# Decay sums of the Mamba heads: from selecting matmuls in PSUM to broadcast loads through DRAM into SBUF

## The chip, the cores and the metric

The kernel runs on one core of one Trainium2 chip, in one launch. The time is the device time of the whole kernel in microseconds, the median of several runs. TensorE (PE in the rows; PEld are its weight loads), VectorE (DVE), ScalarE (ACT), GpSimd (POOL) and SyncE (SP) each work off their own instructions in the order in which the program was built. SP asks for nearly all transfers from memory, ACT for a few.

## The reference

Two layers of a decoder trunk on 256 tokens of width 1024: first a hybrid of gated linear attention and sparse attention and a dense SwiGLU, then a Mamba-2 mixer and eight SwiGLU experts of which each token takes two. The change lies in the Mamba mixer. Of it, this matters:

```
dt = jax.nn.softplus(dt.astype(jnp.float32) + dt_bias)
A = -jnp.exp(a_log.astype(jnp.float32))
a = (dt * A).reshape(B, NC, Q, G, R).transpose(0, 3, 4, 1, 2)
cum = jnp.cumsum(a, axis=-1)
seg = cum[..., :, None] - cum[..., None, :]
L = jnp.exp(jnp.where(causal, seg, -jnp.inf))
cb = jnp.einsum('bclgn,bcsgn->bgcls', Cc, Bc)
y_diag = jnp.einsum('bgcls,bgrcls,bcsgrp->bclgrp', cb, L, xdt)
```

There are 32 heads in four groups of eight. For each head, the running sum cum of its decays is wanted along the tokens on every partition, so that the differences seg of all pairs of tokens can be made. The kernel works in chunks of 128 tokens, two of them, which gives the same y.

## The kernel before

**Stages.** The hybrid mixer runs to about 175 us of the profiled execution, the dense SwiGLU to 378, the Mamba stage to some 600, then the experts. Their first matmul (L1313) starts at 608.8 and they take the rest of the time.

**Weights.** Every weight comes as a tile of 1 MB named raw, asked for by SP at L238 in load(). The tiles form a ring: pool raw_p, to which raw2 is added ahead of the dense stage and raw3 ahead of the experts. A load waits until the tile of one round earlier has been read. Up to the experts, split() makes of each half of a tile a rounded high part wh (ACT, L252) and the remainder wl (DVE, L253), and a product takes three matmuls: wh with the high part of the activations (L267), with their low part (L268), wl with the high part (L269).

**The Mamba stage.** At its start, L963 to L968 make cum, a tile of 32 heads x 256 tokens named fo. L970 to L974 store it as a high and a low part, chl, and make pick. For each of the four groups g of heads, s_proj(g) computes three pairs of projections (each pair in a PSUM bank pa), runs a conv over them (conv(): ACT L986, then three rows on DVE, L988), then the pairs of projections for the gate zs, two tiles, and the activations of xbc (L1019) and zs (L1021), each behind a load of ACT's function table. s_core(g) runs over j = 0 to 3, two heads each. cums(j) puts their running sums on all partitions: two matmuls at L1052 that pick a row of chl, into a PSUM bank pb. ACT reads that bank for seg (four activations, L1066) and for fo (L1069) and takes the exponential of seg (L1070), DVE multiplies both (L1073, L1075), TensorE makes y of them in six matmuls 64 x 128 (L1080 to L1082), DVE adds and multiplies with zs (L1083, L1085). After j = 3 comes the norm of the group: the square y on ACT (L1088), four matmuls (L1091), a copy ms (L1093), one matmul (L1096) and the scaling of y (L1101). L1031, L1032 and L1042 are the first matmuls of the next group's core. outs() runs the output projection on finished groups: y_split() makes hh on ACT (L1115) and yl on DVE (L1116), out_proj() 128x512 matmuls with them.

**What sets the order.** The string SSM_ORDER gives the order in which the steps of these generators are written (p is s_proj, c is s_core). A scheduler then orders each engine's instructions on its own estimates of their times, under the dependences and the free buffers. So an edit at one place can move instructions of all engines of a stage.

Of the kernel before, what the change touches and what calls it, by code (L numbers as in the profile page):

```python
# [8 lines left out]
F32 = mybir.dt.float32  # L9
BF16 = mybir.dt.bfloat16  # L10
F32R = mybir.dt.float32r
# [5 lines left out]
D, T, KD = 1024, 256, 8  # L17
# [168 lines left out]
def trunk_kernel(ctx: ExitStack, tc: tile.TileContext, d: dict, out: bass.AP):  # L186
# [10 lines left out]
    def pbank(tag):  # L197
        return ps_p.tile([128, 512], F32, name=tag, bufs=4 if tag == "pa" else 2)
# [16 lines left out]
    def K(n):  # L215
        s, w = _CS[n]
        return cs[:, s:s + w]
# [679 lines left out]
        dgs = [g[1] for g in dgs]  # L897


    raws.append((ctx.enter_context(tc.tile_pool(name="raw2", bufs=3, side="right")), 3))  # L900
    late = ctx.enter_context(tc.tile_pool(name="late", bufs=1, side="right"))
    px = ctx.enter_context(ExitStack())
    part_p = px.enter_context(tc.tile_pool(name="part", bufs=2))
# [49 lines left out]
    with ExitStack() as sx:  # L953
# [13 lines left out]
        cum = sw.tile([32, T], F32, name="fo")  # L967
        V.tensor_tensor_scan(cum, resets(sw, 32, T, 128, "seg"), dx_, 0.0, op0=OP.mult, op1=OP.add)  # L968

        chl = sp.tile([64, T], F32R, name="chl")  # L970
        S.copy(chl[:32], cum)
        V.tensor_sub(chl[32:], cum, chl[:32].bitcast(F32))
        pick = sp.tile([64, 32], F32R, name="pick")
        S.copy(pick, K("sel32")[:64])  # L974
        dtd = sw.tile([32, 128], F32, name="ms", bufs=1)
        act(dtd, cum[:, :128], AF.Exp, bias=cum[:, 127:128], scale=-1.0)
        V.tensor_mul(dtd, dtd, dtv[:, :128])
# [49 lines left out]
        def s_core(g):  # L1027
# [18 lines left out]
                                 tk[:, i, 8 * g:8 * g + 8, None].to_broadcast([128, 8, 64]))  # L1046

            def cums(j):
                pcu = pbank("pb")
                for e in range(2):  # L1050
                    hh = 8 * g + 2 * j + e
                    PE.matmul(pcu[:, e * T:(e + 1) * T], pick[:, hh:hh + 1].to_broadcast([64, 128]), chl,  # L1052
                              start=True, stop=True)
                return pcu

            y = xT
            pcu = cums(0)
# [3 lines left out]
            for j in range(4):  # L1061
                h0 = 8 * g + 2 * j
                sg = sw.tile([128, 2, 2, 128], F32, name="seg")
                for e in range(2):
                    for c in range(2):
                        act(sg[:, e, c], pcu[:, e * T + c * 128:e * T + (c + 1) * 128], AF.Relu,  # L1066
                            bias=tk[:, 2 + c, h0 + e:h0 + e + 1], scale=-1.0)
                fo = sw.tile([128, 2, 128], F32, name="fo")
                act(fo, pcu.rearrange("p (e n) -> p e n", e=2)[:, :, 128:], AF.Exp)  # L1069
                act(sg, sg, AF.Exp, scale=-1.0)  # L1070
                if j < 3:
                    pcu = cums(j + 1)
                V.tensor_mul(sg.rearrange("p e c n -> p e (c n)"), sg.rearrange("p e c n -> p e (c n)"),  # L1073
                             cbm[:, 0:2].rearrange("p c n -> p (c n)")[:, None, :].to_broadcast([128, 2, 256]))
                V.tensor_mul(fo, fo, cbm[:, 2:3].to_broadcast([128, 2, 128]))  # L1075
                yield
                py = pbank("pc")
                for e in range(2):
                    o_, cc = slice(64 * e, 64 * e + 64), slice(128 * j + 64 * e, 128 * j + 64 * e + 64)
                    PE.matmul(py[o_, :128], xd[:, 0, cc], sg[:, e, 0], start=True, stop=True)  # L1080
                    PE.matmul(py[o_, 128:T], xd[:, 1, cc], sg[:, e, 1], start=True, stop=False)
                    PE.matmul(py[o_, 128:T], xd[:, 2, cc], fo[:, e], start=False, stop=True)  # L1082
                V.scalar_tensor_tensor(y[:, j], xT[:, j], P("dsk")[:, 4 * g + j:4 * g + j + 1], py[:, :T],  # L1083
                                       op0=OP.mult, op1=OP.add)
                V.tensor_mul(y[:, j], y[:, j], zs[:, j])  # L1085
                yield
# [98 lines left out]
    ax.close()  # L1185


    raws.append((ctx.enter_context(tc.tile_pool(name="raw3", bufs=7, side="right")), 7))
    with ExitStack() as mx:
        mp = mx.enter_context(tc.tile_pool(name="moe", bufs=1))  # L1190
        mw = mx.enter_context(tc.tile_pool(name="moew", bufs=2))
# [463 lines left out]
```

## Time and profile before

| | us |
|---|---|
| three runs | 1455.31, 1457.79, 1457.96 |
| median | 1457.79 |
| profiled execution, whole | 1458.05 |
| its span | 1456.0 |
| TensorE busy in the span | 1420.0 (98%) |
| DVE, ACT busy | 561.1 (39%), 437.5 (30%) |
| moved by DMA | 493.66 MB, mean 339 GB/s |

All times in the rows are us from the start of the span, unless ns is written. A row in order of time gives start, duration, engine, line, operation, output<-input with shapes and the number of instructions (x4); in brackets stands the idle time ahead and what ended it. Two rows of one engine may overlap, since its instructions are pipelined: what one costs in a chain is the distance from its start to the next one's. A row of a table by stretches gives the stretch, its length, then busy time and instructions of PE, PEld, DVE, ACT and POOL, then the granted TensorE clock (1.00 is 2.4 GHz, 0.50 is 1.2 GHz), the share of the DMA engines' time and GB/s. A matmul that stands in TensorE's queue and waits may count as busy, so that the distances of starts tell more than the share.

### The profile page before, as it was taken

To read this page: it belongs to the slowest core of one execution; us is meant where nothing else is said; L and a number is where in the kernel's file an instruction comes from. 1 tells how busy PE (TensorE), PEld (TensorE's weight loads), DVE (VectorE), ACT (ScalarE), POOL (GpSimd) and SP (SyncE) were. 2 spreads that over 40 slices of the span, in tenths; PEclk is the share of its full clock that TensorE was granted. 3 is DMA by queue.
4 is the path that set the end of the run, shared out by engine and by line. 5 is a ranking of instruction groups with operands and counts; after the bars stand their busy time and mean duration, and the time that the engine had idled before them with its cause. 6 is when DMAs were issued, how large, how long until landed. Compare 5 with 4: busy or idle time off the path is not lost. (4 is left out here: it accounts for less than half of the span.)

```text
span 1456.0 us, 28571 instructions
## 1 busy us (share of the span) xinstructions
PE 1420.0 (98%) x12257; PEld 808.6 (56%) x12257; DVE 561.1 (39%) x1096; ACT 437.5 (30%) x859; POOL 2.8 (0%) x11
## 2 busy tenths in 40 slices
PE   7999999999999999999999999999999999999996
PEld 6866699999799987633433333333334333333322
DVE  6888588875678778610110011010110110100101
ACT  5577454444577686311100011000001000000002
POOL 0000000000000000000000000000000000000000
PEclk9989999999999999999999999999999999999998
DMA  9876788986643433799999999999999999999994
GB/s 382 350 264 244 296 300 328 376 300 242 242 145 121 170 132 129 278 408 348 356 411 421 419 420 420 419 421 420 420 420 421 419 420 420 420 420 420 420 421 182
DMA packets 68964, 493.66 MB, mean 339 GB/s; under 512 B 7648, under 2 KB 7904, under 8 KB 9568
## 3 DMA queue, kind: packets, MB, share of 16 engines
q1 hardware_dynamic: 68544, 491.25, 84.2%
q8 instruction: 98, 1.61, 0.4%
q10 hardware_dynamic: 288, 0.52, 0.1%
q14 instruction: 34, 0.28, 0.0%
HBM read 490.70 MB, written 1.05 MB: 338 GB/s over the span
## 5 line engine op out<-in xcount | busy, mean ns | idle before, releaser
L1313 PE MATMUL pa<-raw,gx 128*32 128x512 f32 (+1 forms) x5120 | 506.6, 540 | 0.0
L1313 PEld LDWEIGHTS pa<-raw,gx 128*32 128x32 f32 x5120 | 167.0, 110 | 300.1 <-issue 262.5
L1313 PE MATMUL pb<-raw,at 128*32 128x512 f32 x2240 | 252.6, 594 | 0.5 <-ACT at L1348 0.5
L1481 DVE TENSOR_TENSOR sg<-sg,pa 128x256 f32<-128x256 f32 (+1 forms) x80 | 31.0, 387 | 476.5 <-ACT sg L1480 474.8
L253 DVE TENSOR_TENSOR wl<-raw,wh 128x1024 fp32r<-128x1024 f32 (+1 forms) x155 | 185.3, 1203 | 58.4 <-ACT wh L252 58.2
L252 ACT CAST wh<-raw 128x1024 fp32r<-128x1024 f32 (+1 forms) x155 | 158.9, 1035 | 121.0 <-PE pb L268 53.0
L1313 PEld LDWEIGHTS pb<-raw,at 128*32 128x32 f32 x2240 | 70.7, 110 | 152.3 <-issue 147.4
L1480 ACT ACTIVATE sg<-pa 128x256 f32<-128x256 f32 (+1 forms) x80 | 28.5, 357 | 348.5 <-PE pa L1313 348.5
L267 PE MATMUL pa<-hh,wh 128*128 128x256 f32 (+1 forms) x392 | 113.6, 292 | 1.4 <-ACT hh L380 0.6
L268 PE MATMUL pa<-hl,wh 128*128 128x256 f32 (+1 forms) x392 | 112.8, 288 | 0.8 <-DVE hl L386 0.8
L269 PE MATMUL pa<-hh,wl 128*128 128x256 f32 (+1 forms) x392 | 112.5, 288 | 0.0
L267 PE MATMUL pb<-hh,wh 128*128 128x256 f32 (+1 forms) x360 | 102.1, 284 | 1.9 <-ACT hh L380 1.9
L268 PE MATMUL pb<-hl,wh 128*128 128x256 f32 (+1 forms) x360 | 102.4, 285 | 0.1
L269 PE MATMUL pb<-hh,wl 128*128 128x256 f32 (+1 forms) x360 | 102.1, 284 | 0.0
L1348 ACT COPY at<-pc 128x512 f32<-128x512 f32 (+2 forms) x32 | 17.5, 545 | 262.6 <-PE pb L1313 135.1
L281 DVE SCALAR_TENSOR_TENSOR junk<-raw,scb 128x1024 bf16<-128x1024 f32 x72 | 87.7, 1218 | 1.7 <-DMA raw<-in_hyb_mod_dram 1.1
L267 PEld LDWEIGHTS pa<-hh,wh 128*128 128x128 f32 (+1 forms) x392 | 75.0, 192 | 5.4 <-issue 1.8
L268 PEld LDWEIGHTS pa<-hl,wh 128*128 128x128 f32 (+1 forms) x392 | 75.6, 193 | 2.1 <-DVE hl L386 0.9
L269 PEld LDWEIGHTS pa<-hh,wl 128*128 128x128 f32 (+1 forms) x392 | 75.3, 193 | 0.8 <-DVE gu L629 0.3
L267 PEld LDWEIGHTS pb<-hh,wh 128*128 128x128 f32 (+1 forms) x360 | 68.6, 191 | 2.9 <-ACT hh L380 2.1
L268 PEld LDWEIGHTS pb<-hl,wh 128*128 128x128 f32 (+1 forms) x360 | 68.7, 191 | 1.2 <-DVE hl L386 0.8
L269 PEld LDWEIGHTS pb<-hh,wl 128*128 128x128 f32 (+1 forms) x360 | 68.6, 191 | 0.3
(432 smaller groups left out, 1471.6 us busy)
## 6 DMA issues: line engine op xcount, KB each, us to landing
raw<-in_e_gu_dram SPq DMA_DIRECT2D x192, 1024.0 KB, 18.4
raw<-in_e_dn_dram SPq DMA_DIRECT2D x112, 1024.0 KB, 19.4
raw<-in_e_gl_dram SPq DMA_DIRECT2D x32, 1024.0 KB, 17.8
raw<-in_d_gu_dram SPq DMA_DIRECT2D x22, 1024.0 KB, 7.8
raw<-in_s_in_dram SPq DMA_DIRECT2D x20, 1024.0 KB, 4.8
raw<-in_hyb_mod_dram SPq DMA_DIRECT2D x12, 1024.0 KB, 9.4
raw<-in_ssm_mod_dram SPq DMA_DIRECT2D x12, 1024.0 KB, 6.9
raw<-in_d_dn_dram SPq DMA_DIRECT2D x11, 1024.0 KB, 8.3
```

What stands on the lines that cost most here:

```text
L252: hi_last[0] = S.copy(hi[:, :n], r)
L253: lo_last[0] = V.tensor_sub(lo[:, :n], r, hi[:, :n].bitcast(F32))
L267: PE.matmul(ps, a[0], b[0], start=start, stop=False, **kw)
L268: PE.matmul(ps, a[0], b[1], start=False, stop=False, **kw)
L269: return PE.matmul(ps, a[1], b[0], start=False, stop=stop, **kw)
L281: V.scalar_tensor_tensor(jk, r[:, q * D:(q + 1) * D], 1.0, scb, op0=OP.mult, op1=OP.mult, accum_out=macc[m][:, 2 * j + q:2 * j + q + 1])
L1313: up_last[0] = PE.matmul(ps[32 * j:32 * j + 32, :rhs.shape[1]], lhs, rhs, start=start, stop=stop)
L1348: (V.tensor_copy if i else S.copy)(at[:, i:i + n].rearrange("p a n -> p (a n)"), pt_[:, :n * 128])
L1480: last = act(sg[:, r, :w], pg[r][:, :w], AF.Silu)
L1481: V.tensor_mul(sg[:, r, :w], sg[:, r, :w], pg[r][:, w:2 * w])
```

## The change

cum is written once to a tile dr in DRAM and read back, four heads at a time, as a tile cb of 128 partitions x 1024 elements in which every partition holds the same four running sums. There are eight such loads of 512 KB into two buffers; ACT asks for the write and for all loads, the first two at the start, one more after each odd j. seg and fo read cb in SBUF in place of the bank pb. chl, pick and the 32 matmuls of cums go. raw2 has two tiles for three (eight tiles of 1 MB in the ring up to the experts for nine), raw3 eight for seven (sixteen as before in the experts).

```diff
-    raws.append((ctx.enter_context(tc.tile_pool(name="raw2", bufs=3, side="right")), 3))
+    raws.append((ctx.enter_context(tc.tile_pool(name="raw2", bufs=2, side="right")), 2))
...
-        chl = sp.tile([64, T], F32R, name="chl")
-        S.copy(chl[:32], cum)
-        V.tensor_sub(chl[32:], cum, chl[:32].bitcast(F32))
-        pick = sp.tile([64, 32], F32R, name="pick")
-        S.copy(pick, K("sel32")[:64])
+        dr = sx.enter_context(tc.tile_pool(name="dr", bufs=1, space=bass.MemoryType.DRAM)).tile([32, T], F32, name="dr")
+        S.dma_start(dr, cum)
+        cbs = []
+
+        def cum_load():
+            i = len(cbs)
+            if i < 8:
+                cbs.append(sp.tile([128, 4 * T], F32, name="cb", bufs=2))
+                S.dma_start(cbs[i], dr[4 * i:4 * i + 4].rearrange("h n -> (h n)")[None, :].to_broadcast([128, 4 * T]))
+
+        cum_load()
+        cum_load()
...
             def cums(j):
-                pcu = pbank("pb")
-                for e in range(2):
-                    hh = 8 * g + 2 * j + e
-                    PE.matmul(pcu[:, e * T:(e + 1) * T], pick[:, hh:hh + 1].to_broadcast([64, 128]), chl,
-                              start=True, stop=True)
-                return pcu
+                return cbs[2 * g + j // 2][:, j % 2 * 2 * T:(j % 2 + 1) * 2 * T]
...
                 act(sg, sg, AF.Exp, scale=-1.0)
+                if j % 2:
+                    cum_load()
                 if j < 3:
                     pcu = cums(j + 1)
...
-    raws.append((ctx.enter_context(tc.tile_pool(name="raw3", bufs=7, side="right")), 7))
+    raws.append((ctx.enter_context(tc.tile_pool(name="raw3", bufs=8, side="right")), 8))
```

Line numbers after the change are up to 7 higher: L988 becomes L995, L1066 to L1070 become L1068 to L1072, L1080 to L1096 become L1084 to L1100, L1115 becomes L1119. The built program shows that the order of the instructions in the Mamba stage moves too. Numbers behind a tile's name tell buffers apart; they differ between the two programs.

**DVE in the conv of the last group.** pa_5353 and pa_5444 are two of its three PSUM banks, wl_5617 is the first low part of the weights for the gate's projections that follow. Before:

```order
L988 SCALAR_TENSOR_TENSOR xbc_5351<-pa_5353,pc_69,xbc_5351 128x253
L988 SCALAR_TENSOR_TENSOR xbc_5351<-pa_5444,pc_69,xbc_5351 128x255
L253 TENSOR_TENSOR wl_5617<-raw_5614,wh_5616 128x1024
L988 SCALAR_TENSOR_TENSOR xbc_5351<-pa_5353,pc_69,xbc_5351 128x255
L988 SCALAR_TENSOR_TENSOR xbc_5351<-pa_5444,pc_69,xbc_5351 128x254
L988 SCALAR_TENSOR_TENSOR xbc_5351<-pa_5353,pc_69,xbc_5351 128x254
L988 SCALAR_TENSOR_TENSOR xbc_5351<-pa_5444,pc_69,xbc_5351 128x253
L988 SCALAR_TENSOR_TENSOR xbc_5351<-pa_5353,pc_69,xbc_5351 128x253
L1073 TENSOR_TENSOR seg_5600<-seg_5600,cbm_5423 128x512
L988 SCALAR_TENSOR_TENSOR xbc_5351<-pa_5444,pc_69,xbc_5351 128x255
```

After, with pa_5340, pa_5428 and pa_5505 as the three banks and wl_5597 as that low part:

```order
L995 SCALAR_TENSOR_TENSOR xbc_5338<-pa_5428,pc_69,xbc_5338 128x255
L995 SCALAR_TENSOR_TENSOR xbc_5338<-pa_5340,pc_69,xbc_5338 128x254
L995 SCALAR_TENSOR_TENSOR xbc_5338<-pa_5428,pc_69,xbc_5338 128x254
L995 SCALAR_TENSOR_TENSOR xbc_5338<-pa_5340,pc_69,xbc_5338 128x253
L995 SCALAR_TENSOR_TENSOR xbc_5338<-pa_5428,pc_69,xbc_5338 128x253
L995 SCALAR_TENSOR_TENSOR xbc_5338<-pa_5505,pc_69,xbc_5338 128x254
L1089 TENSOR_TENSOR xbc_4920<-xbc_4920,zs_4921 128x256
L995 SCALAR_TENSOR_TENSOR xbc_5338<-pa_5505,pc_69,xbc_5338 128x253
L253 TENSOR_TENSOR wl_5597<-raw_5594,wh_5596 128x1024
L253 TENSOR_TENSOR wl_5625<-raw_5594,wh_5624 128x1024
```

The low part stood among the rows of the first two banks; now it stands behind the last row but one of the third.

**TensorE where group 2 is handed over to group 3.** hh_4418 and hh_4421 are the activations of the output projection. Before:

```order
L269 MATMUL pa_5964<-wh_5987,yl_5966 128x512
L267 MATMUL pa_5965<-wh_5987,hh_4418 128x512
L268 MATMUL pa_5965<-wl_5988,hh_4418 128x512
L269 MATMUL pa_5965<-wh_5987,yl_5966 128x512
L1091 MATMUL pc_5787<-y_5785,cs_68 32x256 x4
L268 MATMUL pa_5963<-wl_6006,hh_4418 128x512
L269 MATMUL pa_5963<-wh_6005,yl_5966 128x512
L267 MATMUL pa_5964<-wh_6005,hh_4418 128x512
L1096 MATMUL pc_5794<-ms_5792,cs_68 128x256
L1031 MATMUL pc_5808<-xbc_5351 128x256
L1032 MATMUL pc_5808<-xbc_5351 128x128
```

After:

```order
L1084 MATMUL pc_5755<-seg_5743,xd_5414 64x128
L1085 MATMUL pc_5755<-seg_5743,xd_5414 64x128
L1086 MATMUL pc_5755<-fo_5748,xd_5414 64x128
L1095 MATMUL pc_5766<-y_5764,cs_68 32x256 x4
L1100 MATMUL pc_5773<-ms_5771,cs_68 128x256
L1038 MATMUL pc_5787<-xbc_5338 128x256
L1039 MATMUL pc_5787<-xbc_5338 128x128
L1049 MATMUL pc_5795<-cs_68,xbc_5338 128x128 x4
L267 MATMUL pa_5929<-wh_5938,hh_4421 128x512
L268 MATMUL pa_5929<-wl_5939,hh_4421 128x512
L267 MATMUL pa_5930<-wh_5938,hh_4421 128x512
```

L1091 stood in a row of wide matmuls of the output projection, 28 of them behind the last L1082; its counterpart L1095 now follows the last L1086 at once, and the wide matmuls begin behind L1100 and L1049.

**ACT at the same place.** zs_5352 and zs_5339 are the gate of group 3, y_5785 and y_5764 the squares of group 2. Before:

```order
L1115 CAST hh_4418<-y_4808 128x1024
L1066 ACTIVATE seg_5863<-pb_5840,tk_4089 128x128 x4
L1069 ACTIVATE fo_5868<-pb_5840 128x256
L1070 ACTIVATE seg_5863<-seg_5863 128x512
L252 CAST wh_6021<-raw_6003 128x1024
L1021 ACT_TABLE_LOAD
L1021 ACTIVATE zs_5352<-pa_5613 128x512
L1021 ACTIVATE zs_5352<-pa_5694 128x512
L348 ACT_TABLE_LOAD
L1088 ACTIVATE y_5785<-xbc_4931 128x1024
L1115 CAST hh_4418<-y_5328 128x1024
L1093 COPY ms_5792<-pc_5787 128x256
```

After:

```order
L1068 ACTIVATE seg_5808<-cb_5589,tk_4092 128x128 x4
L1071 ACT_TABLE_LOAD
L1071 ACTIVATE fo_5813<-cb_5589 128x256
L1028 ACT_TABLE_LOAD
L1028 ACTIVATE zs_5339<-pa_5593 128x512
L1028 ACTIVATE zs_5339<-pa_5671 128x512
L348 ACT_TABLE_LOAD
L1092 ACTIVATE y_5764<-xbc_4920 128x1024
L1072 ACTIVATE seg_5808<-seg_5808 128x512
L1068 ACTIVATE seg_5836<-cb_5589,tk_4092 128x128 x4
L1097 COPY ms_5771<-pc_5766 128x256
L1071 ACTIVATE fo_5841<-cb_5589 128x256
```

The cast hh for the output projection stood ahead of the gate and the square; now it follows them (two rows below the last one shown), and seg of group 3 stands ahead of them, with three table loads among these rows for two.

## Rows read from the trace of the kernel before

**Rows 1.** Table by stretches (columns as told above): Mamba, experts' first part, experts' long part.

```profile
510.00:552.00 42.00, 42.00 (x300) 36.23 (x298) 32.48 (x60) 35.33 (x61) 0.00 (x0) 1.00 0.35 125
611.00:740.00 129.00, 129.00 (x1411) 48.25 (x1407) 16.51 (x63) 14.85 (x37) 0.00 (x0) 1.00 0.96 376
780.00:1440.00 660.00, 651.21 (x6383) 232.28 (x6379) 66.86 (x152) 56.90 (x134) 0.00 (x0) 1.00 1.00 415
```

**Rows 2.** Waits of SP's DMA queue, 611 to 740 us: line, releaser, us, times, longest.

```profile
SPq L238 <- PE pa L1313: 82.0, 35, 9.8
```

**Rows 3.** TensorE in order of time around a pair of L1052 among projections.

```profile
513.74 0.28 PE L269 MATMUL pa<-hh,wl 128*128 128x256 f32 x1
513.95 0.50 PE L1052 MATMUL pb<-chl,pick 64*128 64x256 f32 x2
514.38 0.39 PE L267 MATMUL pa<-hh,wh 128*128 128x256 f32 x1
514.60 0.28 PE L268 MATMUL pa<-hl,wh 128*128 128x256 f32 x1
```

**Rows 4.** TensorE in order of time, group 2's last matmuls and L1091.

```profile
538.49 0.38 PE L1082 MATMUL pc<-fo,xd 128*64 128x128 f32 x2
538.80 0.50 PE L1052 MATMUL pb<-chl,pick 64*128 64x256 f32 x2
539.23 0.50 PE L267 MATMUL pa<-wh,hh 128*128 128x512 f32 x1
...
546.54 0.64 PE L1091 MATMUL pc<-y,cs 128*32 128x256 f32 x8
```

**Rows 5.** ACT at the stage's start; chain of waits; DMA issues (KB, us to landing).

```profile
399.80 0.41 ACT L971 CAST chl<-fo 32x256 fp32r<-32x256 f32 x1 [2.53 <-DVE fo L968]
...
1451.43 0.28 ACTq L1552
...
raw<-in_s_dt_dram SPq DMA_DIRECT2D x1, 128.0 KB, 2.2
```

**Rows 6.** ACT, then DVE, in order of time in a group's conv.

```profile
514.89 0.56 ACT L986 ACTIVATE xbc<-pa,pc 128x256 f32<-128x256 f32 x1
...
517.03 2.03 DVE L988 SCALAR_TENSOR_TENSOR xbc<-pa,pc,xbc 128x255 f32<-128x255 f32 x5
...
524.51 1.22 DVE L253 TENSOR_TENSOR wl<-raw,wh 128x1024 fp32r<-128x1024 f32 x1
```

**Rows 7.** ACT in order of time where group 2 is handed over to group 3.

```profile
538.78 1.14 ACT L1066 ACTIVATE seg<-pb,tk 128x128 f32<-128x128 f32 x4
539.79 0.40 ACT L1069 ACTIVATE fo<-pb 128x256 f32<-128x256 f32 x1
540.05 0.66 ACT L1070 ACTIVATE seg<-seg 128x512 f32<-128x512 f32 x1
...
542.96 1.09 ACT L1021 ACTIVATE zs<-pa 128x512 f32<-128x512 f32 x2
544.06 1.28 ACT L348 ACT_TABLE_LOAD   x1
545.35 1.06 ACT L1088 ACTIVATE y<-xbc 128x1024 f32<-128x1024 f32 x1
546.32 1.03 ACT L1115 CAST hh<-y 128x1024 fp32r<-128x1024 f32 x1
547.25 0.36 ACT L1093 COPY ms<-pc 128x256 f32<-128x256 f32 x1
```

**Rows 8.** TensorE in order of time after a pause, and its table by stretches.

```profile
405.84 0.36 PE L267 MATMUL pa<-hh,wh 128*128 128x256 f32 x1 [0.25 <-DVE xbc L988]
...
408.16 0.41 PE L269 MATMUL pa<-hh,wl 128*128 128x256 f32 x1
408.37 0.41 PE L267 MATMUL pa<-hh,wh 128*128 128x256 f32 x1
...
408.00:410.00 2.00, 2.00 (x11) 2.00 (x11) 2.00 (x4) 1.16 (x4) 0.00 (x0) 0.50 0.04 8
```

## The prediction

> **What bounds the kernel now.** I read the table by stretches first: busy time of each engine, granted TensorE clock and DMA share. In the experts' long stretch, 780 to 1440 us, the DMA engines are busy all the time at 415 GB/s. In their first part, 611 to 740 us, TensorE is busy throughout, the DMA at 0.96. In the Mamba stage, shown by its stretch 510 to 552 us, TensorE is busy 42.00 of 42 us while DVE has 32.48, ACT 35.33 and DMA only 0.35 [rows 1]. The waits of the DMA queue come second: from 611 to 740 us SP waits for nothing but TensorE to free a weight tile, 82.0 us under one line [rows 2]. So a shift of the end of the Mamba stage moves the experts' first matmul, the release of their tiles, the loads, and in the end the last one, all by as much; the DMA's 4% of room there is not spare time at the end. What matters is the Mamba stage, where TensorE sets the pace and DVE and ACT have a sixth to a quarter of their time free on the average. An average hides the question here: whether they deliver in time at each place where TensorE asks for something.
>
> **The part removed: 32 matmuls.** cums is called 16 times for two matmuls at L1052. Among projection matmuls, whose starts lie 0.12 us apart, the last one before a pair takes 0.21, the pair 0.43 and the one after it 0.22 [rows 3]: a pair costs 0.43 + 0.09 + 0.10 = 0.62 us. Next to other matmuls of another shape it costs its own 0.43, as in 538.80 to 539.23 [rows 4]. Three pairs stand at the start of the stage, where TensorE waits for DVE anyway: nothing. Eleven stand between 433 and 537 us: 11 x 0.43 = 4.7 to 11 x 0.62 = 6.8; I take 5.5, as most stand beside a change of shape. The two behind 538 give 0.9. Gain 6.4 us, from 5.6 to 8. The casts and the subtraction for chl and pick (0.41 us [rows 5] each) lie in pauses: nothing.
>
> **The part added.** ACT asks for one write of 32 KB and eight broadcast loads of 512 KB. The only ACT ask in the trace holds its queue 0.28 us, and a 128 KB load lands 2.2 us after it was asked for [rows 5]. The write is asked for at about 399.8, so it has landed by 402.3, about where the first load is asked for, behind the copy of tk. What is queued behind these asks are the conv activations, on which TensorE waits there: I take 0.5 us, from nothing to 1.5 (write and load in series). The other six asks come far ahead of their readers; 9 x 0.28 = 2.5 us of ACT. The loads are 4 MB in a stage with a DMA share of 0.35. One raw tile fewer up to the experts: weight tiles land well before they are used, and I put this at zero, with the risk as a rival below. The eighth raw3 tile gives back the slot where SP waits for TensorE: zero.
>
> **The part moved.** This decides. The scheduler has laid out all three engines of the stage anew, and at two places TensorE now stands behind a chain of ACT and DVE with little of its own to do.
>
> First place, the end of the last group's conv. Before, DVE makes the wl for the next projection (L253) in the middle of its conv rows; after, it stands behind all of them. T is the end of the last conv projection. ACT: a weight cast 1.0 us (shape of L1115 [rows 7]), then three conv activations of 0.5 [rows 6]: T + 2.5. DVE, from the last of them: six conv rows of 0.41, the product with zs, as wide, 0.4, one more conv row 0.41, wl 1.2 [rows 6]: 4.5, so wl is there at T + 7.0. TensorE has from T twelve small matmuls and four of 0.12 with changes of shape, about 2 us. It stands 5.0 us; the lower bound 3 is that DVE gets at its rows earlier than the waits allow for, the upper one 5.5.
>
> Second place, group 2 handed over to group 3. Before, TensorE runs 28 wide matmuls of the output projection from 539.2 to 546.5 us, while ACT works off seg, fo, zs, two table loads and the square y; L1091 then starts 0.1 us after y's end [rows 4, 7]. After, those wide matmuls stand behind L1095, L1100 and L1049. ACT's chain begins when TensorE has read seg halfway through the last twelve small matmuls: seg 1.01, table load 1.29, fo 0.26, table load 1.29, zs 1.10, table load 1.29, y 0.97, each from one start to the next [rows 7]: 7.2 us. TensorE has about 0.6 us left to do and stands 6.6. Then L1095, half a microsecond, whose result ACT copies only behind exp 0.55, seg 1.01 and the copy 0.3: TensorE stands 1.3. The first wide matmul needs the cast hh, behind the copy, fo 0.26, exp 0.55 and the cast 0.93: it stands 0.8 beyond the microsecond of L1100 to L1049. The third kind, L269, needs yl, a DVE row of the shape of wl, 1.2 us against 0.7 us of wide matmuls: 0.5. Sum 9.2 us, from 7.5 to 10.5.
>
> The clock: after sparse work and a wait of 0.25 us before 405.84 the granted clock stands at 0.50, the level of 1.2 GHz, in 408 to 410 us, and projection matmuls there start 0.21 us apart [rows 8]. The 3.3 us from 406.8 to 410.1 at that level cost some 1.5 us of work. Behind the first place TensorE has a row of projections, which pay all of it; behind the second it waits for the chain anyway, so I take 0.4. Sum 2.0, from nothing to 4. Smaller changes of order at the start of the dense stage and between earlier groups: 0.5, from nothing to 1.5.
>
> A table load shows 1.28 us in this trace, and the next activation follows at once: zs ends at 544.06, y starts at 545.35 [rows 7]. The Trainium skill, page "ScalarE: Activation LUTs", section "What ACT_TABLE_LOAD costs", adds a drain of some 1.38 us, 2.66 us for each switch. The trace does not show it as lost time on ACT. By the page the three loads of the second place would add 3 x 1.38 = 4.1 us.
>
> **The sum.** -6.4 + 0.5 + 5.0 + 9.2 + 2.0 + 0.5 = +10.8 us on the profiled execution's 1458.05 (span 1456.0 and 2.05 around it), which lies 0.3 above the median of 1457.79: 1468.6, say 1468.5.
>
> **The rivals.**
> 1. Not slower: TensorE never waits at the two places, because ACT and DVE run ahead of it. For it speaks that no wait of a matmul shows between 412 and 596 us before, and DVE has a quarter of its time free. Against it: the chains hang on TensorE's own last matmuls, so ACT cannot begin them earlier, however idle it is; L1091 before followed y by 0.1 us with all its cover. Price: the gain alone, -6.4 + 0.5, about 1452. It decides if the two chains take less than 3 us together. Chance 0.07.
> 2. One place only. Only the second: -6.4 + 0.5 + 9.2 + 0.9 = +4.2, 1462; only the first: -6.4 + 0.5 + 5.0 + 1.6 = +0.7, 1458.5. For it: DVE's rows at the first place may be served earlier than I count. Chance 0.15, of which 0.05 for the first alone.
> 3. The ring of eight tiles starves TensorE on top. For it: every load up to the experts is asked for one tile later; against: DMA share of 0.35 in the Mamba stage. A tile that is late by the 2.5 us that a megabyte takes at 415 GB/s, in four places, gives about 1478. Chance 0.08.
> 4. Every table load holds ACT longer than its row by a drain: three in the second chain, about 1473, inside the range; chance 0.05. The page named above says so.
> That the change doesn't do what it says isn't open: the order has no L1052 matmul left.
>
> **How the numbers follow.** Forecast as summed: 0.65. With the low ends of all terms it is 1458.05 - 8 + 0 + 3 + 7.5 = 1460.5; with the high ends -5.6 + 1.5 + 5.5 + 10.5 + 4 + 1.5 = +17.4, 1475.5. Not all ends come together, so the forecast's own range is 1462 to 1474. The range from 1460 to 1475 takes in the second place alone and the drain; it leaves out rival 1, most of rival 3 and the first place alone, 0.2 in all. A measurement can tell about 0.2% (3 us) from no change. Faster: rival 1, 0.07. Same: the first place alone, 0.06. Slower 0.87.
>
> **What would show it.** In the changed kernel: a wait of L269 for wl at L253 of 2 to 5 us after the last conv; a wait of L1095 for y (L1092) of 6 to 7 us, then short ones of L1100, L267 and L269; ACT without a pause in that chain; the granted clock at 0.50 for some 3 us behind at least one; TensorE otherwise without waits and some 6 us of matmul time less; the first experts' matmul 10 us later and the DMA at 415 GB/s as before. Wrong it is if TensorE's pauses between 412 and 600 us sum to less than 6 us, or if they are there and the first experts' matmul is no later.

## The result

The changed kernel takes 1466.47 us, median of 6 runs (1466.07 to 1468.05), the kernel before 1455.40 in the runs beside it (1451.36 to 1457.96): ratio 1.0077, 95% interval 1.0060 to 1.0095. It is slower by some 11 us; the forecast was 1468.5 in a range from 1460 to 1475. The profiled execution of the changed kernel has a span of 1464.9 us against 1456.0, so 8.9 us more. The early stages of single executions differ by some us, which lies between the two numbers. The forecast of +10.8 us was counted from that profiled execution, so it is to be held against the 8.9.

The trace puts all of it into one stretch. I measure it from the scan of cum on DVE (L968 in both kernels) to the experts' first matmul:

| | scan | first expert matmul | stretch | from there to the end |
|---|---|---|---|---|
| before | 399.09 | 608.8 | 209.7 | 847.2 |
| changed | 398.97 | 617.3 | 218.3 | 847.6 |

The rest behind it is the same to 0.5 us. The table by stretches of the changed kernel, with the columns of [rows 1], shows why:

```profile
510.00:552.00 42.00, 30.52 (x232) 27.78 (x230) 30.88 (x59) 30.00 (x52) 0.00 (x0) 0.84 0.41 142
620.00:750.00 130.00, 130.00 (x1421) 48.48 (x1413) 16.85 (x63) 14.86 (x38) 0.00 (x0) 1.00 0.98 384
790.00:1440.00 650.00, 641.75 (x6300) 229.50 (x6292) 66.91 (x152) 56.53 (x133) 0.00 (x0) 1.00 1.01 419
```

The experts' stretches answer to [rows 1] unchanged: 0.98 and 1.01 of the DMA where 0.96 and 1.00 stood. The first row does not: TensorE busy for 30.52 of 42 us, where it was 42.00, and a mean granted clock of 0.84. TensorE's waits from 395 to 600 us (line, releaser, us in total, times, longest) name the places:

```profile
PE pc L1095 <- ACT y L1092: 7.0, 1, 7.0
PE pa L267 <- DVE xbc L995: 4.1, 2, 2.5
PE pa L269 <- DVE wl L253: 2.1, 1, 2.1
PE pc L1100 <- ACT ms L1097: 0.9, 1, 0.9
```

Before, this list had one line:

```profile
PE pa L267 <- DVE xbc L988: 0.3, 1, 0.3
```

Now it holds 14.1 us, and the forecast chains are among its entries: L1095 for the square y, L269 for the low part wl, L1100 for the copy ms. L267 waits for conv rows twice, 2.50 at the start of the stage and 1.59 at the last conv.

**The hand-over from group 2 to group 3.** ACT, in order of time, the counterpart of [rows 7]:

```profile
537.73 1.28 ACT L1068 ACTIVATE seg<-cb,tk 128x128 f32<-128x128 f32 x4
539.02 1.28 ACT L1071 ACT_TABLE_LOAD   x1
540.32 0.42 ACT L1071 ACTIVATE fo<-cb 128x256 f32<-128x256 f32 x1
540.74 1.28 ACT L1028 ACT_TABLE_LOAD   x1
542.03 1.08 ACT L1028 ACTIVATE zs<-pa 128x512 f32<-128x512 f32 x2
543.12 1.28 ACT L348 ACT_TABLE_LOAD   x1
544.42 1.06 ACT L1092 ACTIVATE y<-xbc 128x1024 f32<-128x1024 f32 x1
```

and TensorE meanwhile, the counterpart of [rows 4]:

```profile
538.18 0.38 PE L1086 MATMUL pc<-fo,xd 128*64 128x128 f32 x2
545.53 1.08 PE L1095 MATMUL pc<-y,cs 128*32 128x256 f32 x8 [6.96 <-ACT y L1092]
547.47 1.22 PE L1100 MATMUL pc<-ms,cs 128*128 128x256 f32 x2 [0.86 <-ACT ms L1097]
...
550.48 0.76 PE L267 MATMUL pa<-wh,hh 128*128 128x512 f32 x1
```

ACT has no pause from 537.73 to the end of y, and TensorE stands from its last L1086 to 545.53. The wide matmuls, which began at 539.23 before, begin at 550.48. In the stretches of 2 us the granted clock falls during the pause and stays at half, the level of 1.2 GHz, while TensorE works off the short chain; from 552 it is full again:

```profile
542.00:544.00 2.00, 0.00 (x0) 0.00 (x0) 0.00 (x0) 1.98 (x4) 0.00 (x0) 0.50 0.81 340
546.00:548.00 2.00, 1.14 (x9) 0.50 (x2) 0.00 (x0) 2.00 (x7) 0.00 (x0) 0.50 0.00 0
552.00:554.00 2.00, 2.00 (x12) 1.69 (x11) 2.00 (x5) 0.00 (x0) 0.00 (x0) 1.00 0.00 0
```

**The last conv.** TensorE in order of time, then DVE:

```profile
521.73 0.36 PE L267 MATMUL pa<-hh,wh 128*128 128x256 f32 x1 [1.59 <-DVE xbc L995]
...
524.27 0.58 PE L269 MATMUL pa<-hh,wl 128*128 128x256 f32 x1 [2.07 <-DVE wl L253]
524.65 0.42 PE L267 MATMUL pa<-hh,wh 128*128 128x256 f32 x1
```

```profile
519.07 3.29 DVE L995 SCALAR_TENSOR_TENSOR xbc<-pa,pc,xbc 128x255 f32<-128x255 f32 x8
522.28 0.41 DVE L1089 TENSOR_TENSOR xbc<-xbc,zs 128x256 f32<-128x256 f32 x1
522.62 0.47 DVE L995 SCALAR_TENSOR_TENSOR xbc<-pa,pc,xbc 128x253 f32<-128x253 f32 x1
523.01 2.35 DVE L253 TENSOR_TENSOR wl<-raw,wh 128x1024 fp32r<-128x1024 f32 x2
```

The low part for the gate's projections is made at 523.01, behind eight conv rows, the product with zs and one more; L269 waits for it. Behind that pause the matmuls start 0.21 to 0.22 us apart up to 527.21 and 0.12 behind it, and the granted clock is 0.50 from 524 to 526: it has fallen here too.

### The profile page after: what moved, and what is told of

It reads as the page before. It is cut to its first block, busy times and chain, and to the rows that moved or that the text cites. A ratio compares the mean times of both kernels' runs of the same rounds, so it can differ in the third digit from the quotient of the medians.

```text
span 1464.9 us, 28529 instructions
## 1 busy us (share of the span) xinstructions
PE 1412.8 (96%) x12225; PEld 804.2 (55%) x12225; DVE 560.9 (38%) x1095; ACT 442.4 (30%) x859; POOL 2.8 (0%) x11
## 3 DMA queue, kind: packets, MB, share of 16 engines
HBM read 494.89 MB, written 1.08 MB: 339 GB/s over the span
## 5 line engine op out<-in xcount | busy, mean ns | idle before, releaser
L267 PE MATMUL pa<-hh,wh 128*128 128x256 f32 (+1 forms) x392 | 113.1, 293 | 5.0 <-DVE xbc L995 4.1
L269 PE MATMUL pa<-hh,wl 128*128 128x256 f32 (+1 forms) x392 | 112.2, 288 | 2.1 <-DVE wl L253 2.1
L267 PE MATMUL pb<-hh,wh 128*128 128x256 f32 (+1 forms) x360 | 101.9, 284 | 1.9 <-ACT hh L380 1.9
L269 PE MATMUL pb<-hh,wl 128*128 128x256 f32 (+1 forms) x360 | 102.4, 284 | 0.0
L267 PEld LDWEIGHTS pa<-hh,wh 128*128 128x128 f32 (+1 forms) x392 | 75.2, 193 | 8.6 <-ACT wh L252 3.4
L269 PEld LDWEIGHTS pa<-hh,wl 128*128 128x128 f32 (+1 forms) x392 | 75.4, 193 | 2.8 <-DVE wl L253 2.3
L267 PEld LDWEIGHTS pb<-hh,wh 128*128 128x128 f32 (+1 forms) x360 | 68.6, 191 | 2.9 <-ACT hh L380 2.1
L269 PEld LDWEIGHTS pb<-hh,wl 128*128 128x128 f32 (+1 forms) x360 | 68.9, 191 | 0.3
```

The lines of the kernel that those rows point to most:

```text
L267: PE.matmul(ps, a[0], b[0], start=start, stop=False, **kw)
L269: return PE.matmul(ps, a[1], b[0], start=False, stop=stop, **kw)
```

## The experiments

All are compared with the kernel before on the same chip. The early stages differ between executions by up to 5 us: from 80 to 100 us the granted clock was 0.83 in the trace of before, 0.74 in that of the changed kernel, 1.00 in that of e3_hand, and the scan lay between 394 and 399 us. So I read the stretch from the scan to the first expert matmul first, and the whole time with its interval beside it.

The stretch of a single trace is not exact either. In some executions the granted clock falls at the start of the Mamba stage, in others it doesn't; the table gives its mean from 400 to 420 us. e8_order and e12_order_5 are the same kernel, and its stretch is 204.0 us with 1.00 and 205.1 with 0.91. So runs of the same granted clock are compared where it matters: before has 0.91, and e1_ring8, which differs from it in two pool sizes only, has 1.00.

| run | stretch, us | clock, 400 to 420 us | rest, us | ratio to before (interval) |
|---|---|---|---|---|
| before | 209.7 | 0.91 | 847.2 | |
| changed | 218.3 | 0.91 | 847.6 | 1.0077 (1.0060 to 1.0095) |
| e1_ring8 | 208.5 | 1.00 | 847.8 | 0.9996 (0.9982 to 1.0010) |
| e2_ask_sp | 217.2 | 0.91 | 848.9 | 1.0072 (1.0048 to 1.0096) |
| e3_hand | 216.7 | 0.91 | 847.8 | 1.0045 (1.0028 to 1.0061) |
| e4_conv | 218.6 | 0.91 | 847.8 | 1.0072 (1.0045 to 1.0100) |
| e5_double | 217.5 | 1.00 | 847.5 | 1.0051 (1.0031 to 1.0071) |
| e6_one_cb | 220.5 | 0.91 | 847.8 | 1.0080 (1.0055 to 1.0105) |
| e7_both | 219.6 | 0.91 | 849.2 | 1.0074 (1.0048 to 1.0100) |
| e8_order | 204.0 | 1.00 | 848.9 | 0.9978 (0.9960 to 0.9996) |
| e9_before_order | 212.6 | 1.00 | 847.1 | 1.0040 (1.0021 to 1.0059) |
| e10_order_act | 210.0 | 0.91 | 848.1 | 1.0009 (0.9995 to 1.0022) |
| e11_order2 | 207.6 | 0.83 | 848.9 | 0.9990 (0.9977 to 1.0003) |
| e12_order_5 (e8 again) | 205.1 | 0.91 | 849.2 | 0.9989 (0.9975 to 1.0003) |

My theory A: the removal is a gain, but the instructions were laid out anew, so that TensorE pauses behind chains of ACT and DVE. The rivals: B, the shorter ring; C, the loads and their asks.

### Is it the ring or the loads?

**e1_ring8.** The kernel before with the pools of the change.

```diff
-    raws.append((... tile_pool(name="raw2", bufs=3, side="right")), 3))
+    raws.append((... tile_pool(name="raw2", bufs=2, side="right")), 2))
...
-    raws.append((... tile_pool(name="raw3", bufs=7, side="right")), 7))
+    raws.append((... tile_pool(name="raw3", bufs=8, side="right")), 8))
```

> The kernel before with only the two pool sizes of the change: raw2 2 for 3 tiles, raw3 8 for 7. Theory A (the changed kernel is slower because TensorE pauses in the Mamba stage behind chains of ACT and DVE in a new order): no difference, ratio to before 0.998 to 1.002, no wait of a Mamba matmul over 1 us. Rival B (the shorter ring up to the experts starves TensorE or shifts the experts' loads): slower by 6 us or more.

No difference in the whole, and the stretch is no longer than before. Rival B falls: eight tiles are enough up to the experts.

**e6_one_cb.** The changed kernel with one load for all heads. It leaves out seven loads, so the decays of the other heads are wrong, and it serves for its time alone.

```diff
-            if i < 8:
+            if i < 1:
...
-                return cbs[2 * g + j // 2][:, ...]
+                return cbs[0][:, ...]
```

> The changed kernel with only the first of the eight loads: all heads read the first four heads' running sums, so seven loads and asks are left out and the decays of the other heads are wrong. Theory A (pauses of TensorE from the new order): the order keeps both pauses, so within 2 us of the changed kernel, 218.3 us from the scan to the experts' first matmul there. Rival C (loads and asks cost the time): back to 209 us or less in that stretch.

```profile
PE pc L1095 <- ACT y L1092: 7.0, 1, 7.0
...
```

All four waits are those of the changed kernel to the digit, with seven loads fewer, and no time is won. So rival C falls for the loads: none of the 8.6 us is theirs. The stretch is even 2.2 us longer, and that is the clock. These are the rows of the changed kernel and of e6_one_cb, the scan 3.2 us earlier in the second:

```profile
520.00:540.00 20.00, 14.91 (x120) 14.21 (x118) 17.04 (x28) 13.37 (x24) 0.00 (x0) 0.91 0.54 184
520.00:540.00 20.00, 15.71 (x116) 15.34 (x116) 14.61 (x21) 11.93 (x16) 0.00 (x0) 0.83 0.53 173
```

Behind the same wait for wl the matmuls start 0.21 us apart for 13 of them in the changed kernel and for 28 here, which is 1.4 us; the rest is the half clock at the first wide matmuls, which start 0.43 us apart here from 549.25 to 550.96 and 0.23 apart there. What a pause costs behind it thus differs between executions of the same order.

**e2_ask_sp.** The loads asked for by SP.

```diff
-                S.dma_start(cbs[i], dr[...]...)
+                nc.sync.dma_start(cbs[i], dr[...]...)
```

> The changed kernel with the eight loads asked for by SP instead of ACT (the write stays on ACT). Theory A: the pauses at the last conv and at the hand-over from group 2 to 3 stay (some 4 us, and 7 + 2 us); only the pause at the stage's start, 2.5 us before the first projection behind the conv, gets shorter by 1 to 2 us. So 0 to 3 us faster than the changed kernel, still 6 us or more slower than before. Rival C (asks on ACT hold up ACT and cost the time): back to before, some 10 us faster than the changed kernel.

```profile
PE pc L1095 <- ACT y L1092: 7.0, 1, 7.0
PE pa L267 <- DVE xbc L995: 2.8, 2, 1.6
```

The two later places stay as they were; at the start TensorE waits 1.3 us less. So the asks on ACT are not the cause of the two pauses. What they do at the start shows on DVE, here with SP as asker:

```profile
401.71 1.23 DVE L253 TENSOR_TENSOR wl<-raw,wh 128x1024 fp32r<-128x1024 f32 x1 [1.62 <-ACT wh L252]
402.85 4.76 DVE L995 SCALAR_TENSOR_TENSOR xbc<-pa,pc,xbc 128x255 f32<-128x255 f32 x12
```

The conv rows follow the low part at once. In the changed kernel two other copies stand between them (see the start, below), so who asks moves the order of DVE; e10_order_act shows the same.

### What moved the order?

**e7_both.** The changed kernel with chl, pick and the matmuls kept: seg reads the loaded tile, fo the bank.

```diff
...
+                pcu = pbank("pb")
+                ...
+                    PE.matmul(pcu[:, e * T:(e + 1) * T], pick[...].to_broadcast([64, 128]), chl, ...)
+                pcus.append(pcu)
                 return cbs[2 * g + j // 2][...]
...
-                act(fo, pcu.rearrange(...)[:, :, 128:], AF.Exp)
+                act(fo, pcus[-1].rearrange(...)[:, :, 128:], AF.Exp)
```

> The changed kernel with chl, pick and the 32 matmuls kept beside the loads: seg reads the loaded tile, fo the PSUM bank as before. If the pauses come from the matmuls' absence, so that TensorE is too fast for the order, they go and the stretch from the scan to the experts' first matmul is some 210 us. If they come from seg no longer being tied to the two PSUM banks, the wait for y (L1107 here) stays with 4 to 7 us and the matmuls fall partly into the pauses: 216 to 222 us.

```profile
PE pc L1107 <- ACT y L1104: 4.3, 1, 4.3
PE pb L1065 <- DVE xbc L1101: 1.8, 1, 1.8
```

With all 32 matmuls back the pause at the hand-over stays. Two pairs of them now stand in it, so it shows as two waits, 1.8 and 4.3 us, together 0.9 less than 7.0, which is about what two pairs take. The stretch is no shorter than in the changed kernel. So the missing matmuls did not open this pause. The pause at the last conv is another matter: L269 waits for wl 0.3 us here, and no wait of L267 shows, so for that place the run excludes nothing. For the hand-over, with e1, e2 and e6 excluding pools, asker and loads, what is left of the change is that seg reads a tile in SBUF and no longer one of the two PSUM banks. That is a conclusion by exclusion; why the scheduler then puts seg of group 3 ahead of the cast hh isn't shown by any run.

### What are the pauses worth?

**e3_hand.** y_split(0), which makes hh and yl for the first output projections, written ahead of group 3's core.

```diff
             y = xT
             pcu = cums(0)
+            if g == 3:
+                y_split(0)
...
-                if j % 2 == 0:
+                if j % 2 == 0 and len(hhs) <= j // 2:
                     y_split(j // 2)
```

> The changed kernel with y_split(0), the split for the output projection's first group, written ahead of group 3's core instead of behind it. The wide matmuls of the output projection then stand between group 2's last small matmuls and L1095's counterpart again. Theory A: the 7 us wait for the square y goes; smaller waits (1 to 3 us each, for the cast hh and the subtraction yl, and at the router) come behind; 2 to 6 us faster than the changed kernel. Rival B or C (ring, loads, asks): no change.

```profile
PE pc L1086 <- DVE seg L1079: 2.3, 1, 2.3
PE pa L269 <- DVE wl L253: 2.1, 1, 2.1
PE pa L269 <- DVE yl L1123: 1.5, 1, 1.5
PE pc L1159 <- DVE br L1157: 1.5, 1, 1.5
```

The wait of 7.0 us is gone, but three new ones of 2.3, 1.5 and 1.5 have come, all for DVE; the waits at the start and at the last conv stay. The stretch gains 1.6 us, a little under the 2 to 6 expected. Some 1 us more is hidden by the clock: behind the last conv 24 matmuls run at half of it here, 13 in the changed kernel. The whole time of 1460.69 us looks like 5.8 gained, but in the traces 4.9 of the difference lie ahead of the scan.

**e4_conv.** The weights of the gate's first projections split ahead of the third conv.

```diff
+                if i == 2:
+                    zw = list(halves(d["s_in"][5 * g + 3]))
                 for q in range(2):
                     conv(xbc[:, 2 * i + q], pq[q], cs_[2 * i + q])
...
-                for j, w in enumerate(halves(d["s_in"][5 * g + 3 + i])):
+                for j, w in enumerate(halves(d["s_in"][5 * g + 3 + i]) if i else zw):
```

> The changed kernel with the weights of the gate's first projections split ahead of the third conv in s_proj, so that the low part wl stands ahead of that conv's rows on DVE. Theory A: the pause of some 4 us at the last conv becomes smaller, the order behind it changes with it; the wait for y goes but the router's matmul waits some 5 us; 2 to 5 us faster than the changed kernel. Rival B or C: no change.

```profile
PE pc L1158 <- DVE br L1156: 4.4, 1, 4.4
...
PE pc L1086 <- ACT seg L1070: 1.2, 1, 1.2
PE pc L1088 <- DVE fo L1081: 1.1, 1, 1.1
```

A miss: both old pauses are gone or small, and yet the stretch is as long as in the changed kernel. The router's matmul now waits 4.4 us, and the waits of group 2's small matmuls add 2.4. In place of the pauses taken away the new order has others.

**e8_order.** Both edits, SP as asker, and another SSM_ORDER.

```diff
-SSM_ORDER = "m p c p c c c c p c c p c c c c p c c c p p c p c c c p c p c c c c c p c p c p c c p c c p c c c c c c c c t c c c c c c c c c c c"
+SSM_ORDER = "m p c p c c c c p c c p c c c p c c c c p p c c p p c c c p c c c c p c c p c p c c p c p c c c c c c c t c c c c c c c c c c c c c"
```

> The changed kernel with its order repaired: loads asked for by SP, y_split(0) ahead of group 3's core, the gate's first weights split ahead of the third conv, and another SSM_ORDER (later p and earlier t steps). Theory A: no wait of TensorE over 2 us between 412 and 600, and the gain of the removed matmuls comes through: 203 to 209 us from the scan to the experts' first matmul against 209.7 before and 218.3 in the changed kernel; whole time 1 to 6 us under before. Rival: the memory path itself costs time; then it stays above 214 us.

```profile
PE pa L269 <- DVE yl L1125: 1.3, 1, 1.3
PE pa L267 <- DVE xbc L995: 1.2, 1, 1.2
PE pa L267 <- ACT hl L1124: 0.3, 1, 0.3
```

With 3.0 us of waits left the stretch is 204.0 us: 14.3 less than in the changed kernel, 5.7 less than before. Against e1_ring8, with the same clock at the start, it is 4.5. So the memory path itself is a gain in this order, and the changed kernel's order had eaten it more than twice over. The whole is 0.9978 of before.

**e12_order_5.** The same kernel, five rounds.

> e8_order once more with five rounds, to see whether it is faster than the kernel before. e8_order gave 0.9978 (0.9960 to 0.9996). The stretches give 204.05 + 848.9 against 209.71 + 847.2, so 4 us less, 0.997. Expected ratio 0.996 to 0.999; if e8's three rounds were luck, 1.000.

0.9989, interval 0.9975 to 1.0003. Both measurements are on the faster side, some 2 to 3 us, but the second interval takes in no change, so this is just at what can be told. With the clock at the start alike the traces give 4.5 us (against e1_ring8) and 4.7 us (against before) in the stretch, of which the rest behind it takes back 1.1 to 2.0; why the rest is longer in the kernels with SP as asker (848.9 to 849.2) and in e7_both is open.

**e9_before_order.** The kernel before with e8's three edits of order.

> The kernel before (matmuls, PSUM, nine tiles) with the three edits of e8_order that move instructions: y_split(0) early, the gate's first weights early, the same SSM_ORDER. It tells whether e8's gain is one of order alone. If the removed matmuls are the gain, this kernel is no faster than before in the stretch from the scan to the experts' first matmul (209.7 us), rather 1 to 5 us slower, since that order was chosen for the other kernel. If order alone is the gain, it comes out at 203 to 206 us.

Slower by 2.9 us in the stretch, and by 4.1 against e1_ring8 with the same clock. So e8's gain is not one of order alone. That order was chosen for the other kernel, though; whether a search would find a better order for the kernel before as well, no run tells.

**e10_order_act.** e8_order with ACT as asker again.

> e8_order with the loads asked for by ACT again, as in the change. In e2_ask_sp against the changed kernel the asker was worth 1 us. Here the same 1 us by the asks themselves; more, up to 5 us (204.05 to 209), if the asks on ACT move the order of the conv rows at the start and of later steps.

```profile
PE pa L267 <- DVE xbc L995: 2.5, 1, 2.5
PE pc L1088 <- DVE seg L1081: 2.4, 1, 2.4
```

5.9 us lost against e8_order, 4.9 against e12_order_5 with the same clock at the start, and so more than the 1 us of e2: the start's wait is back at 2.5, and a wait of 2.4 for seg has come in group 3. The asker matters here by what it does to the order.

**e11_order2.** Another SSM_ORDER, with SP as asker and the edit of e4_conv, without that of y_split.

> A second repaired order: loads asked for by SP, the gate's first weights ahead of the third conv, y_split(0) where the changed kernel has it, another SSM_ORDER with one step of the output projection early. Expected 202 to 206 us from the scan to the experts' first matmul (204.05 in e8_order), the whole 1450 to 1454 us, under before by 2 to 5 us.

207.6 us, outside the 202 to 206 expected; the whole cannot be told from before. The list of waits holds only 1.4 us, less than e8_order's, so waits aren't what it is short of. The granted clock from 400 to 420 us was 0.83 in this trace: 0.17 x 20, up to 3.4 us, of which e8_order lost nothing.

### What is a pair of matmuls worth?

**e5_double.** The kernel before with each L1052 matmul done twice.

```diff
+                    for _ in range(2):
-                    PE.matmul(pcu[...], pick[...].to_broadcast([64, 128]), chl, start=True, stop=True)
+                        PE.matmul(pcu[...], pick[...].to_broadcast([64, 128]), chl, start=True, stop=True)
```

> The kernel before with each of the 32 matmuls of cums done twice into the same bank, so 64. The time from the scan of cum to the experts' first matmul was 209.7 us in the trace of before. If a pair costs 0.43 (its own time) to 0.62 us (with the changes of shape) where TensorE has no pause, as in the sum of the prediction, the second copies cost 13 x 0.43 = 5.6 us, at most 8, in that stretch and in the whole. If the matmuls lie in pauses or cost only their stream of 0.1 us each, 0 to 3 us.

```profile
PE pc L1153 <- DVE br L1151: 3.0, 1, 3.0
```

The stretch is 7.7 us longer than before, within what I expected, and 8.9 longer than e1_ring8's with the same clock at the start, which is above it. The reason given doesn't hold either: 3.0 us of it are a new wait at the router, since the order moved, and the half clock follows that wait. Summing the distances from each of these matmuls' starts to the next start gives 7.3 us for the 32 of before and 10.6 for the 64 here: a second copy costs 0.10 us, not 0.22, as in the other case that I had named. So half or more of a pair's price (0.43 us alone, 0.62 among projections) is paid for the first matmul behind another shape, and a copy of the same matmul doesn't pay it again. The run is no measure of what the removal saves.

## Why the prediction was right

The direction and the two places were right, and the mechanism behind them: TensorE stands behind chains of ACT and DVE, and the end moves with it. The size came out because errors cancel. One by one:

**What sets the end.** Right: the experts' first matmul is 8.4 us later, the end 8.9, the rest 847.2 and 847.6.

**The first place.** Forecast: wl at T + 7.0 and 5.0 us of pause. The last conv projection starts at 517.28, so T is about 517.4, and wl can be used at 524.27, T + 6.9; but TensorE's own sixteen matmuls (each of the twelve small ones stands twice in the trace) took 3.2 us, not 2, and the pause is 1.59 + 2.07 = 3.7. The chain was right; the term was 1.3 too large, because I made TensorE's own work too short. A part of the pause, 1.59 us at L267, lies earlier than forecast; conv rows of the same chain on DVE end it.

**The second place.** Forecast 6.6 + 1.3 + 0.8 + 0.5 = 9.2. Measured 6.96 and 0.86, and no wait shown at L267 or at L269. The first is longer than forecast: from seg to the end of y ACT took 7.65 us, from 537.73 to 545.38, not 7.2. A part is that seg from SBUF is slower: four take 1.29 us up to a table load where before they took 1.16 (531.58 to 532.74), against my reading that the source made no difference. The other part is the overlap of two activations, which I had counted and which is not there ahead of a table load. The later waits are gone because TensorE had the half clock, as the next point tells.

**The clock.** Forecast 2.0, mostly behind the first place. Measured there: 13 distances from 524.27 to 527.21, 2.9 us for 1.6, so 1.4; in e6_one_cb the same order paid twice that, so this size is in part luck. Behind the second I took 0.4; L1095 alone shows 1.08 us where [rows 4] has 0.64, and from L1100 to the first wide matmul 3.0 us pass for work whose distances before sum to 1.4: about 2.1. So 3.5 in all, and the term was mis-sized. Of the 2.1 some 0.8 us would have been waiting at the full clock (an estimate from the rows: ACT copies ms at 547.07 and ends the cast hh at 549.19, whatever TensorE's clock); the other 1.3 I had held to be hidden by the chain, and they weren't.

**The start.** Forecast 0.5, for asks that hold up ACT. Counted from the scan, TensorE's first projection behind the conv starts 1.3 us later than before (its wait is longer by 2.3, since two pairs of matmuls that stood ahead of it are gone). ACT was not held up. ACT, then DVE, then TensorE there:

```profile
401.70 0.83 ACTq L978 DMA_DIRECT2D cb<-dr  x2
...
402.58 1.93 ACT L993 ACTIVATE xbc<-pa,pc 128x256 f32<-128x256 f32 x4
```

```profile
403.70 0.16 DVE L322 COPY mac_moe<-pc 128x4 f32<-128x4 f32 x1
404.59 0.16 DVE L322 COPY mac_moe<-pc 128x4 f32<-128x4 f32 x1 [0.73 <-PE pc L321]
404.87 4.76 DVE L995 SCALAR_TENSOR_TENSOR xbc<-pa,pc,xbc 128x255 f32<-128x255 f32 x12
```

```profile
407.05 0.36 PE L267 MATMUL pa<-hh,wh 128*128 128x256 f32 x1 [2.50 <-DVE xbc L995]
```

ACT's conv activations start at 402.58, as before (402.57), though ACT's queue asks twice ahead of them (some 0.4 us each, not 0.28). On DVE two copies for the experts' modulation (L322), the second of which waits for TensorE, now stand ahead of the conv rows, which start at 404.87. With SP as asker (e2_ask_sp) the copies don't stand there, and the projection starts 6.8 us after the scan, as before. So the asks cost this time through the order of DVE, not by holding up ACT: the size lay within the bounds, the way was another.

**The matmuls removed.** Forecast 6.4, from 5.6 to 8. It can't be read directly. By difference in the changed kernel it is 7.7 (the table below). From the repaired order it is some 6 us: e12_order_5 against before, with the same clock at the start, is 4.7 shorter with 1.6 more of waits behind the start. So the term was about right. One reading behind it was wrong: of the three pairs put into the pause at the start, the third stands behind it, among projections (410.84 in the trace of before), and cost some 0.6 us.

**The errors cancel.** All terms, in us, measured in the stretch:

| term | forecast | measured |
|---|---|---|
| first place | 5.0 | 3.7 |
| second place | 9.2 | 7.8 |
| clock | 2.0 | 3.5 |
| start | 0.5 | 1.3 |
| other changes of order | 0.5 | none seen |
| matmuls removed | -6.4 | -7.7, by difference |
| sum | +10.8 | +8.6 |

The pauses at the two places were forecast 2.7 too large, the clock 1.5 too small. That the median lies only 2 us under the forecast is in part luck.

**The rivals.** The first, no pauses, fell with the list of waits; the second, one place only, too. The third, the ring, fell with e1. The fourth, a drain at each table load, can be read from ACT's rows above: each of the three loads takes 1.28 us, and the next activation starts 1.29 to 1.30 us after the load's start; ahead of a load only the 0.1 us is lost by which two activations overlap otherwise. The Trainium skill, page "ScalarE: Activation LUTs", section "What ACT_TABLE_LOAD costs", gives 2.66 us for each switch, some 1.38 of it a drain. By that page the chain would have taken 3 x 1.38 = 4.1 us more than it did, which is an estimate from the page's figure. The measurement decides: 1.3 us each in this chain.

## What to carry to other kernels

An edit that takes a dependence away can let the scheduler lay out a whole stage anew; read the built order at the places where the bound engine asks for something, and add up the chain it would stand behind, before counting the gain. Such a pause costs its length and then, in these traces, the half clock for the work right behind it, 13 to 28 matmuls at the last conv. When a change loses by order, repair the order before giving it up: here a loss of 11 us became a gain of some 2, at the edge of what the runs can tell. And before a difference of a few us is put down to an edit, compare the granted clock of the two traces.

## What the runs showed of the hardware that I had not expected

Reading the running sums from SBUF rather than from a PSUM bank made ACT's seg slower, not faster. The changed kernel's row for all 64 (line, form, count; busy, mean ns; idle before):

```profile
L1068 ACT ACTIVATE seg<-cb,tk 128x128 f32<-128x128 f32 x64 | 20.6, 393 | 0.7 <-PE pc L1085 0.7
```

The mean was 376 ns before, and 395 in e7_both, where seg reads SBUF with all matmuls back. A group of four takes 1.17 us to the start of fo instead of 1.01; seg, fo and the exponential together take 2.02 us (559.57 to 561.59) instead of 1.80 (558.54 to 560.34), some 3 us more of ACT over the stage's sixteen rounds.

A matmul of 64 rows by 256 columns that repeats the one ahead of it costs 0.10 us (e5_double); a single one between matmuls of other shapes takes three times that, 0.31 us from start to start (530.31 to 530.62 in the trace of before).

How long the half clock lasts behind a pause isn't fixed by the program: behind the same wait of 2.07 us for wl at the last conv it held for 13 matmuls in the changed kernel, 14 in e2_ask_sp, 24 in e3_hand and 28 in e6_one_cb.

The eight broadcast loads of 512 KB land 3.9 us (median) after they are asked for and the write of 32 KB after 1.5 us, and in e6_one_cb leaving out seven of the loads wins no time.
